# Sums of x's squares by ScalarE from a token-major copy of x, with h's row tiles and the memory's factors as jobs of their own

## The chip, the cores and the metric

The kernel runs on one core of one Trainium2 chip. The metric is the device time of the whole program in microseconds (us); several runs of a program are told by their median. TensorE (PE) does the matmuls, VectorE (DVE), ScalarE (ACT) and GpSimd (POOL) the elementwise work, and SyncE (SP) issues nearly all DMA transfers.

## What is computed

Two layers of an encoder trunk on x of 512 tokens by 1024 features, with 256 memory tokens beside it:

```python
for l in range(DEPTH):
    h = _rmsnorm(x, norm_g[l])
    u = h @ w_in[l]                 # one projection, split into the inputs of four head groups
    y_a = _hgrn2_branch(...)        # gated linear recurrence, both directions
    y_b = _window_attention(...)
    y_c = _mlstm_branch(...)
    y_d = _memory_attention(d_q, d_z, _rmsnorm(mem, mem_norm_g[l]), w_mem_kv[l])
    x = x + jnp.concatenate([y_a, y_b, y_c, y_d], axis=-1) @ w_out[l]
return _rmsnorm(x, final_norm_g)

def _rmsnorm(x, g):
    y = xf * lax.rsqrt(jnp.mean(xf * xf, axis=-1, keepdims=True) + EPS)
    return y * g
```

The change concerns the first layer's `_rmsnorm(x)` and `_rmsnorm(mem)`: the sum of squares over the 1024 features of each token, and what is made of it.

## The kernel before

Every float32 matrix product is done as three matmuls on a pair of parts, hi (the value rounded by a copy) and lo (the rest): hi·hi, hi·lo, lo·hi. Weights come from HBM in blocks of 512 rows by 256 columns (tile `wr`, three buffers); ACT copies a block to `wh`, DVE subtracts to `wl` (three buffers each), in `load_w`. x is loaded feature-major, as eight tiles `in_xT` of 128 features by 512 tokens (`xs`).

The program starts in `start()`. The normalised h needs a factor per token that isn't known until all of x has been squared, so the first projections run on h0, which is x times the gain without the factor, and the factor is multiplied on when the result is taken out of PSUM. For each of the eight feature tiles k the loop loads x and a piece of the first weight block, makes hi and lo of both, and issues six matmuls of the q projection into the two PSUM banks `o` (the tiles `pts`), 48 in all. In the same loop the squares are made: GpSimd squares the even tiles, ACT the odd ones, GpSimd and DVE add the eight squared tiles up into one (`plus`). Then a job R, written as a generator `rest()`, goes on:

- four matmuls of the summed tile with a column of ones (`add_squares`) give the token sums in PSUM (`tr`); `rms4` turns them into factors on ACT and DVE, `diag` puts them on a diagonal `dg`;
- after a yield, `spread` multiplies `dg` with a matrix of ones, so that every partition holds all the factors, and ACT copies this to R. DVE then multiplies the two q tiles by R, and `norm_k` makes h itself for k = 0 to 7: one multiplication by R (DVE for even k, GpSimd for odd k), hi by ACT, lo by DVE;
- the sums of the memory's squares were made by ACT from a token-major copy (`in_mem`); their `diag` and, after another yield, their `spread` into `Rm` close the job.

The forget gates of head group A are the first work that needs R. `gates()` does two projections of h0, one into the banks `s` (d = 1), one into `pj` (d = 0), and each result is multiplied by R on DVE before ACT's sigmoids. They are followed by `values()`, the first projection that needs h, and the two heads of `mix_A`: seven levels of a tree, each with small matmuls into the banks `s`, an update of K2 on GpSimd, one of Q2 on DVE, a masked copy on DVE. A job `memn` (`mem_norm`, `mem_kv`) multiplies the feature-major memory (`in_memT`) by gain and `Rm` on DVE and splits it into hi and lo.

Order: each engine runs its instructions in the order of its own stream, and SP its transfers likewise. `Weave` holds the jobs: the main line calls `tick` every few matmuls, which adds the time that they take by its plan, and a job whose due time (the `after` of its spawn, then the second number of each yield) has come runs a step. A framework then orders the instructions of each engine, where `tc.high_priority()` lets a piece go ahead; in the loop of `start()` the program's order is kept. So numbers such as `R_LAT` decide where in the streams a job's instructions stand.

Of the kernel before, what the change touches and what calls it, by code (L numbers as in the profile page):

```python
# [9 lines left out]
AF = mybir.ActivationFunctionType  # L10
# [4 lines left out]
P = 128  # L15
# [66 lines left out]
R_LAT0, R_LAT = 6000, 3500  # L82
M_LAT, M_LAT2 = 20000, 2500


def pack(inp):
# [18 lines left out]
    out = {"xT": inp["x"][0].T.reshape(8, P, T), "memT": inp["mem"][0].T.reshape(8, P, 256).transpose(1, 0, 2),  # L105
# [91 lines left out]
def trunk(tc, a, dbg=None, mark=lambda s: None):  # L197
# [6 lines left out]
    with es:  # L204
# [265 lines left out]
        def add_squares(ps, sq, n, first, last):  # L470

            for c in range(n):
                gmm(ps[:, c:c + 1], sq[:, c * P:(c + 1) * P], ones[:, 0:1], first and c == 0, last)

# [71 lines left out]
        jobM, mem0 = [], []  # L546
# [126 lines left out]
        def group_A(l, h, pr, yT, between=None, before=None, raw=None):  # L673
# [54 lines left out]
            if pr == 0:  # L728
                gates()
                if raw is not None:  # L730
                    jobM.append(wv.spawn("memn", mem_norm(), after=M_LAT))
# [464 lines left out]
        def mem_norm():  # L1196
            yield 0, 0
            mem0.append(mem_kv(0))
            next(mem0[0])
            yield 0, 0  # L1200
# [199 lines left out]
        def start():  # L1400
# [15 lines left out]
            sums = ptr()  # L1416
            pts = [po(), po()]
            R = a2([512])
            sqs = []

            def plus(e, i, j):
                e.tensor_tensor(sqs[i], sqs[i], sqs[j], ALU.add)
            for k in range(8):
# [19 lines left out]
                for b, pt in enumerate(pts):  # L1443
# [3 lines left out]
                    mm(pt, wl[:, c], hi, start=False, stop=(k == 7))  # L1447

            ms = a["mem"].rearrange("b (c p) d -> p (b c) d", p=P)
            ssm = sm([2], "ssm", 1)  # L1450
            mt = [u4([D]) for _ in range(2)]
            es2.close()
            for c in range(2):
                sy.dma_start(mt[c], ms[:, c])
# [117 lines left out]
```

## Time and profile before

| | |
|---|---|
| Median of 3 runs | 1136.97 us (1136.57 to 1139.35) |
| The profiled execution: its own time | 1137.1 us |
| The profiled execution: its span | 1135.3 us |
| PE busy | 1079.4 us, 95% |
| DVE busy | 795.3 us, 70% |
| ACT busy | 538.3 us, 47% |
| POOL busy | 243.4 us, 21% |
| Chain that ended last | PE 71%, DVE 18%, ACT 3% of the span |

The span is the time from the first to the last record; 1.8 us of the execution's own time lie around it. A time in a view counts from the start of the span. Busy shares average over very different stages: in the first 2.5% of the span PE is busy for six tenths, later for nearly all of it. What an edit is worth is to be read from the stage in which it lies. A PE that is busy can also be busy at half its pace: the clock granted is a column of its own.

### The profile page before, as it was taken

The page shows a single profiled execution, that of the slowest core. Times are in us where ns is not written, and L with a number is a line of the kernel's source. Part 1 is how long each engine was busy: PE and PEld are TensorE (multiplying, and loading weights), DVE is VectorE, ACT ScalarE, POOL GpSimd, SP SyncE. Part 2 cuts the span into 40 slices and gives each one's busy share as a digit, 9 for nine tenths or more (in the row PEclk, how much of TensorE's full clock was granted, in tenths as well). Part 3 has the DMA queues.
Part 4 walks back from the last instruction along what each step waited for, and adds up shares of the span by engine and source line. Part 5 has one row for each costly group of instructions (what it writes and reads, how often), then busy time and mean ns, then how long its engine had stood idle before and what let it go on. Part 6 is the DMA issues. An engine that isn't in the chain of part 4 may idle for free.

```text
span 1135.3 us, 22387 instructions
## 1 busy us (share of the span) xinstructions
PE 1079.4 (95%) x8886; PEld 968.2 (85%) x8886; DVE 795.3 (70%) x1759; ACT 538.3 (47%) x1138; POOL 243.4 (21%) x276
## 2 busy tenths in 40 slices
PE   6889999989999999999999999999899999999997
PEld 4778988989888888788788889889888788989997
DVE  7799536787486768777464786377968759688664
ACT  5545335666443534344564433376654353442443
POOL 4252000231142123111020241012304311230200
PEclk9999999999999999999999999999999999999998
DMA  7222134111221444422434221311121233362211
GB/s 255 77 94 76 57 104 158 59 57 45 88 75 58 108 107 122 148 76 92 134 128 142 81 67 58 98 62 56 58 75 57 76 108 98 103 195 77 74 38 74
DMA packets 34783, 105.41 MB, mean 93 GB/s; under 512 B 4360, under 2 KB 7816, under 8 KB 34680
## 3 DMA queue, kind: packets, MB, share of 16 engines
q1 hardware_dynamic: 33960, 101.57, 28.4%
q0 software_dynamic: 720, 2.42, 0.6%
q8 instruction: 70, 1.15, 0.4%
q14 instruction: 33, 0.27, 0.1%
HBM read 99.72 MB, written 4.26 MB: 92 GB/s over the span
## 4 chain that ended last, share of the span: by engine, by line
PE 71%; DVE 18%; ACT 3%; issue 2%; DMA 1%; POOL 0%; SPq 0%; DVEq 0%; ACTq 0%; POOLq 0%
PE pj L248 33%; PE pj L251 23%; DVE a L142 7%; DVE u L142 5%; PE o L248 4%; DVE wl L142 3%; PE s L248 3%; PE s L251 2%; ACT wh L142 1%; PE tr L857 1%; PE o L251 1%; ACT u L142 1%; ACT a L142 1%; DVE rq_t L142 1%; PE tr L1290 1%
## 5 line engine op out<-in xcount | busy, mean ns | idle before, releaser
L251 PE MATMUL pj<-wh,u 128*128 128x256 f32 x1984 | 390.7, 287 | 3.2 <-ACT u L142 1.2
L248 PE MATMUL pj<-u,wh 128*128 128x512 f32 (+1 forms) x1216 | 376.8, 391 | 1.0 <-ACT a L142 0.8
L251 PEld LDWEIGHTS pj<-wh,u 128*128 128x128 f32 x1984 | 317.0, 190 | 8.2 <-ACT u L142 2.4
L142 DVE TENSOR_TENSOR wl<-wr,wh 128x1024 fp32r<-128x1024 f32 (+1 forms) x162 | 215.4, 1330 | 135.8 <-ACT wh L142 135.3
L251 PE MATMUL pj<-wl,u 128*128 128x256 f32 x992 | 280.7, 283 | 0.0
L248 PEld LDWEIGHTS pj<-u,wh 128*128 128x128 f32 x1216 | 219.2, 190 | 42.5 <-ACT a L142 1.2
L248 PE MATMUL pj<-u,wl 128*128 128x512 f32 (+1 forms) x608 | 234.0, 385 | 1.8 <-DVE wl L142 1.8
L142 ACT CAST wh<-wr 128x1024 fp32r<-128x1024 f32 (+1 forms) x162 | 164.1, 1014 | 151.1 <-PE pj L248 88.0
L251 PEld LDWEIGHTS pj<-wl,u 128*128 128x128 f32 x992 | 188.3, 190 | 0.8 <-issue 0.3
L248 PEld LDWEIGHTS pj<-u,wl 128*128 128x128 f32 x608 | 115.4, 190 | 25.3 <-DVE wl L142 2.0
L142 POOL TENSOR_TENSOR u<-u,a 128x512 f32<-128x512 f32 (+1 forms) x64 | 93.2, 1464 | 133.0 <-PE s L251 53.5
L142 POOL TENSOR_SCALAR u<-u,rB 128x256 f32<-128x256 f32 (+1 forms) x64 | 37.3, 595 | 232.9 <-DVE rB L142 132.5
L142 POOL TENSOR_TENSOR u<-u,u 128x512 f32<-128x512 f32 x16 | 29.3, 1830 | 210.9 <-DVE a L142 125.0
L248 PE MATMUL pj<-wh,u 128*128 128x256 f32 (+1 forms) x320 | 62.8, 287 | 0.0
L142 DVE TENSOR_TENSOR u<-u,a 128x512 f32<-128x512 f32 (+1 forms) x56 | 50.2, 897 | 15.9 <-PE s L251 13.5
L248 PE MATMUL o<-u,u 128*128 128x129 f32 (+1 forms) x384 | 50.2, 275 | 1.9 <-DVE dnC L142 1.9
L248 PEld LDWEIGHTS o<-u,u 128*128 128x128 f32 x384 | 48.2, 191 | 4.4 <-issue 2.4
L248 PEld LDWEIGHTS pj<-wh,u 128*128 128x128 f32 x320 | 51.0, 188 | 0.7 <-issue 0.5
L251 PEld LDWEIGHTS s<-u,u 128*32 128x32 f32 (+1 forms) x1760 | 27.4, 115 | 28.1 <-issue 19.3
L251 PE MATMUL s<-u,u 128*32 128x32 f32 (+2 forms) x1760 | 35.0, 207 | 17.2 <-DVE a L142 13.6
L142 ACT COPY u<-u 128x512 f32<-128x512 f32 x40 | 27.0, 684 | 40.7 <-DVE u L142 22.8
L248 PE MATMUL pj<-wl,u 128*128 128x256 f32 (+1 forms) x160 | 45.3, 283 | 0.0
(213 smaller groups left out, 1494.3 us busy)
## 6 DMA issues: line engine op xcount, KB each, us to landing
wr<-in_wpk SPq DMA_DIRECT2D x154, 512.0 KB, 3.3
u<-in_xT SPq DMA_DIRECT2D x16, 256.0 KB, 4.6
u<-rdr SPq DMA_DIRECT2D x16, 256.0 KB, 4.5
u<-gdr SPq DMA_DIRECT2D x16, 192.0 KB, 5.8
u<-in_memT SPq DMA_DIRECT2D x4, 512.0 KB
xd<-u POOLq DMA_DIRECT2D x4, 512.0 KB, 4.8
u<-xd SPq DMA_DIRECT2D x4, 512.0 KB, 5.4
out<-u SPq DMA_DIRECT2D x8, 256.0 KB, 2.0
```

Of the source, the lines that this page charges most:

```text
L142: r = f(*args, **kw)
L248: nc.tensor.matmul(out, l, r, start=start, stop=stop)
L251: nc.tensor.matmul(out, l, r, start=start, stop=stop, skip_group_check=True)
L857: nc.tensor.transpose(pt[:, j * P:(j + 1) * P], pr[e][:, j * P:(j + 1) * P], ident)
L1290: nc.tensor.transpose(pt[:, (2 * t + i) * P:(2 * t + i + 1) * P], pr[:, i, t * P:(t + 1) * P], ident)
```

## The change

1. x is loaded a second time, token-major (`in_x`, four tiles of 128 tokens by 1024 features, 512 KB each), behind the first weight blocks and ahead of `in_mem`.
2. The squares and their additions leave the loop of `start()`, from GpSimd, ACT and DVE. ACT squares the four token-major tiles in `rest()`, and the sum over the features comes out of the same instruction (`accum_out`). The four matmuls with a column of ones are gone.
3. `norm_k` of the eight row tiles of h becomes a job N of its own, with one tile per step, and all eight multiplications by R are on DVE. `group_A` joins N ahead of `go()`.
4. The memory's `diag` is handed to the job `memn`, which does `spread` into `Rm` as its first step.
5. The due times that go with these jobs are others.

```diff
-R_LAT0, R_LAT = 6000, 3500
-M_LAT, M_LAT2 = 20000, 2500
+R_LAT0, R_LAT = 0, 9000
+H_LAT = 1100
+M_LAT, M_LAT2 = 20000, 1500
...
             if pr == 0:
                 gates()
+                wv.join(*jobN)
+                jobN.clear()
                 if raw is not None:
                     jobM.append(wv.spawn("memn", mem_norm(), after=M_LAT))
...
         def mem_norm():
             yield 0, 0
+            spread(jobM.pop(0), Rm)
+            yield 450, M_LAT2
             mem0.append(mem_kv(0))
...
-                sqs.append(a2([512]))
-                if k % 2 == 1:
-                    act.activation(sqs[k], x, AF.Square)
-                    if k < 6:
-                        plus(gp, k - 1, k)
-                else:
-                    gp.tensor_tensor(sqs[k], x, x, ALU.mult)
-                if k == 5:
-                    plus(dve, 0, 2)
-                elif k == 7:
-                    for j in (4, 6, 7):
-                        plus(dve, 0, j)
...
+            for name, ts in (("x", xt), ("mem", mt)):
+                src = a[name].rearrange("b (c p) d -> p (b c) d", p=P)
+                for c, t in enumerate(ts):
+                    sy.dma_start(t, src[:, c])
+
+            def squares(ts, ss):
+                for c, t in enumerate(ts):
+                    act.activation(t, t, AF.Square, accum_out=ss[:, c:c + 1])
             q = [a2([512]) for _ in range(2)]
 
             def rest():
 
+                squares(xt, sst)
                 with tc.high_priority():
-                    add_squares(sums, sqs[0], NC, True, True)
-                    dg = diag(rms4(sums[:, 0:NC]), NC)
-                yield 900, R_LAT
+                    dg = diag(rms4(sst), NC)
+                yield 0, R_LAT
                 with tc.high_priority():
                     spread(dg, R)
                     for b in range(2):
                         dve.tensor_tensor(q[b], pts[b], R, ALU.mult)
-                for k in range(8):
-                    norm_k(xs[k // 2][:, k % 2], k, R, 0, h, gp if k % 2 else dve)
-                for c in range(2):
-                    act.activation(mt[c], mt[c], AF.Square, accum_out=ssm[:, c:c + 1])
-                dg = diag(rms4(ssm, 2), 2)
-                yield 900, M_LAT2
-                spread(dg, Rm)
-                yield 450, 0
+                squares(mt, ssm)
+                jobM.append(diag(rms4(ssm, 2), 2))
+                jobN.append(wv.spawn("N", norms()))
+                yield 900, 0
+
+            def norms():
                 for k in range(8):
-                    norm_k(xs[k // 2][:, k % 2], k, R, 0, h, gp if k % 2 else dve)
+                    norm_k(xs[k // 2][:, k % 2], k, R, 0, h, dve)
+                    yield 0, H_LAT
```

How the streams differ, at three places. The rows are those of one engine in its own order, before and changed; `a_`, `u_` and so on are tiles with running numbers, which differ between the two.

PE where the q projection (`o`) ends and the gate projection d = 1 (`s`) begins; `tr_137` is the product with the column of ones. Before:

```order
L248 MATMUL o_139<-u_8_101,wl_129 128x512
L248 MATMUL s_277<-u_5_98,wh_266 128x512
L248 MATMUL s_277<-u_9_102,wh_266 128x512
L251 MATMUL tr_137<-ones,a_31_145 128x1 x4
L248 MATMUL s_277<-u_5_98,wl_267 128x512
```

and changed:

```order
L249 MATMUL o_138<-u_12_105,wh_128 128x512
L249 MATMUL o_138<-u_8_101,wl_129 128x512
L249 MATMUL s_262<-u_5_98,wh_251 128x512
L249 MATMUL s_262<-u_9_102,wh_251 128x512
L249 MATMUL s_262<-u_5_98,wl_252 128x512
```

The product with the ones, which stood two matmuls into the gate projection, is gone; the `spread` matmul now follows 19 matmuls into that projection, where before it stood 11 in.

DVE from the factors of x on (before: `a_60_322` is their diagonal; `a_30_140` is R, `a_62_335` and the next three are the even tiles' products with R). Before:

```order
L142 TENSOR_TENSOR a_60_322<-cf,rx_57_313 128x512
L142 TENSOR_TENSOR wl_405<-wr_403,wh_404 128x4x256
L142 TENSOR_TENSOR a_42_249<-o_138,a_30_140 128x512
L142 TENSOR_TENSOR a_43_250<-o_139,a_30_140 128x512
L142 TENSOR_TENSOR a_62_335<-u_1_94,a_30_140 128x512
L142 TENSOR_TENSOR a_64_343<-u_2_95,a_30_140 128x512
L142 TENSOR_TENSOR a_66_351<-u_3_96,a_30_140 128x512
L142 TENSOR_TENSOR a_68_359<-u_4_97,a_30_140 128x512
L142 TENSOR_TENSOR wl_411<-wr_409,wh_410 128x4x256
```

and changed (`a_29_139` is R, `s_262` the first gate result, `a_61_331` the diagonal of the memory's factors):

```order
L143 TENSOR_TENSOR a_38_234<-o_137,a_29_139 128x512
L143 TENSOR_TENSOR a_39_235<-o_138,a_29_139 128x512
L143 RECIPROCAL rx_58_322<-rx_58_322 128x2
L143 TENSOR_TENSOR rxv_59_323<-rxv_59_323,rx_58_322 128x2
L143 TENSOR_TENSOR wl_363<-wr_361,wh_362 128x4x256
L143 SCALAR_TENSOR_TENSOR rxt_60_324<-rxv_59_323,rx_58_322 128x2
L143 SCALAR_TENSOR_TENSOR rx_58_322<-rxt_60_324,rx_58_322 128x2
L143 TENSOR_TENSOR a_61_331<-cf,rx_58_322 128x256
L143 TENSOR_TENSOR wl_369<-wr_367,wh_368 128x4x256
L143 TENSOR_TENSOR a_62_333<-s_262,a_29_139 128x512
L143 TENSOR_TENSOR a_63_340<-u_1_94,a_29_139 128x512
L143 TENSOR_TENSOR a_64_350<-u_1_94,a_29_139 128x512
```

The memory's factors, `wl` of two blocks and the first gate result moved ahead of the products of x with R, and those are eight instead of four.

DVE among the levels of `mix_A` (`u_121`, `u_122`, in the change `u_119`, `u_120`: the feature-major memory; updates of Q2 have forms such as 128x128x2x2). Before, ahead of the update by the second level:

```order
L142 TENSOR_TENSOR a_101_520<-a_101_520 128x8
L142 SCALAR_TENSOR_TENSOR u_121_849<-u_121_849,pg,Rm 128x256 x3
L142 TENSOR_TENSOR u_96_494<-u_96_494,a_42_249 128x128x2x2
L142 COPY_PREDICATED a_99_499<-cu,s_679 128x128
L142 TENSOR_TENSOR wl_992<-wr_990,wh_991 128x4x256
L142 TENSOR_TENSOR u_100_519<-u_100_519,a_43_250 128x128x2x2
L142 COPY_PREDICATED a_103_524<-cu,s_729 128x128
L142 SCALAR_TENSOR_TENSOR u_121_849<-u_121_849,pg,Rm 128x256
```

and changed, ahead of the update by the fifth level:

```order
L143 TENSOR_SCALAR rk_938<-ang 128x32
L143 SCALAR_TENSOR_TENSOR u_119_871<-u_119_871,pg,Rm 128x256
L143 SCALAR_TENSOR_TENSOR u_110_696<-a_126_931,pj_698 128x512
L143 TENSOR_TENSOR wl_1221<-wr_1219,wh_1220 128x4x256
L143 SCALAR_TENSOR_TENSOR u_119_871<-u_119_871,pg,Rm 128x256 x3
L143 SCALAR_TENSOR_TENSOR u_120_872<-u_120_872,pg,Rm 128x256 x3
L143 TENSOR_TENSOR u_123_875<-u_119_871,u_121_873 128x1024
L143 SCALAR_TENSOR_TENSOR u_120_872<-u_120_872,pg,Rm 128x256
L143 TENSOR_SCALAR rk_938<-rk_938 128x32
L143 TENSOR_TENSOR u_91_476<-u_91_476,a_92_477 128x16x2x16
```

The products with `Rm` start three levels later; the result that frees the PSUM bank `pj_698` and the block `wl_1221` stand among them. In SP's stream the two transfers of `in_memT` moved two weight blocks back, to behind `wr_1461`.

## Rows read from the trace of the kernel before

**Rows 1.** Busy time by stage: window; PE, PEld, DVE, ACT, POOL; clock, DMA, GB/s.
```profile
23.10:26.50 3.40, 1.51 (x11) 1.07 (x10) 2.71 (x6) 0.00 (x0) 0.00 (x0) 1.00 0.73 219
26.50:31.40 4.90, 4.90 (x15) 3.55 (x15) 2.76 (x11) 1.45 (x4) 0.00 (x0) 0.65 0.34 106
...
43.90:47.00 3.10, 0.13 (x1) 0.02 (x1) 3.10 (x6) 0.00 (x0) 0.00 (x0) 1.00 0.04 13
47.00:51.20 4.20, 4.19 (x12) 3.33 (x13) 1.26 (x3) 3.45 (x5) 0.00 (x0) 0.59 0.36 115
...
65.00:92.00 27.00, 20.36 (x384) 18.50 (x383) 26.86 (x43) 11.62 (x18) 11.81 (x8) 1.00 0.30 99
...
110.00:1135.00 1025.00, 989.15 (x7939) 891.49 (x7937) 701.77 (x1596) 481.88 (x1045) 200.50 (x242) 0.99 0.29 89
```

**Rows 2.** PE's waits up to 110 us: waiter, releaser: sum, times, longest.
```profile
PE s L251 <- DVE a L142: 5.4, 3, 3.4
PE tr L248 <- DVE a L142: 3.0, 1, 3.0
PE tr L251 <- DVE a L142: 1.9, 1, 1.9
```

**Rows 3.** PE in order of time: start, us, instruction, count, idle before.
```profile
13.72 0.39 PE L248 MATMUL o<-u,wl 128*128 128x512 f32 x1
...
22.21 0.40 PE L248 MATMUL o<-u,wl 128*128 128x512 f32 x1
...
22.91 0.39 PE L248 MATMUL o<-u,wl 128*128 128x512 f32 x1
...
26.54 0.48 PE L248 MATMUL s<-u,wl 128*128 128x512 f32 x1
...
56.04 0.28 PE L251 MATMUL pj<-wh,u 128*128 128x256 f32 x1
```

**Rows 4.** DVE and POOL in order of time during the q projection.
```profile
9.12 0.41 DVE L142 TENSOR_TENSOR wl<-wr,wh 128x256 fp32r<-128x256 f32 x1
...
14.02 1.26 DVE L142 TENSOR_TENSOR wl<-wr,wh 128x256 fp32r<-128x256 f32 x1
...
13.51 1.49 POOL L142 TENSOR_TENSOR a<-u 128x512 f32<-128x512 f32 x1
```

**Rows 5.** The same columns as rows 1, for the loads ahead of the memory's.
```profile
11.25:13.50 2.25, 2.25 (x7) 1.71 (x7) 2.25 (x2) 2.25 (x6) 2.17 (x2) 1.00 1.08 393
```

**Rows 6.** ACT and DVE in order of time: squares with sum, factors, R.
```profile
18.84 1.06 ACT L142 ACTIVATE u<-u 128x1024 f32<-128x1024 f32 x1
...
19.80 0.19 ACT L142 ACTIVATION_READ_ACCUMULATOR u<-u 128x1 f32 x1
...
26.72 0.26 ACT L142 ACTIVATE rx<-tr,epst 128x4 f32<-128x4 f32 x1 [6.73 <-PE tr L251]
...
28.29 0.69 DVE L142 TENSOR_TENSOR a<-cf,rx 128x512 f32<-128x512 f32 x1 [0.34 <-DVE rx L142]
...
31.34 0.59 ACT L142 COPY a<-tr 128x512 f32<-128x512 f32 x1 [3.24 <-PE tr L248]
```

**Rows 7.** DVE in order of time with GpSimd idle: lo of h, wl, results.
```profile
40.02 4.71 DVE L142 SCALAR_TENSOR_TENSOR u<-a,pg,u 128x512 fp32r<-128x512 f32 x7
44.66 1.21 DVE L142 TENSOR_TENSOR wl<-wr,wh 128x1024 fp32r<-128x1024 f32 x1
...
46.79 1.27 DVE L142 TENSOR_TENSOR a<-s,a 128x512 f32<-128x512 f32 x2
```

**Rows 8.** POOL, DVE and SP in order of time around the levels of mix_A.
```profile
61.28 2.94 POOL L142 TENSOR_TENSOR u<-u,u 128x512 f32<-128x512 f32 x1 [0.69 <-DVE a L142]
...
63.00 2.29 DVE L142 TENSOR_TENSOR wl<-wr,wh 128x1024 fp32r<-128x1024 f32 x1 [0.73 <-ACT wh L142]
...
75.80 2.17 DVE L142 SCALAR_TENSOR_TENSOR u<-u,pg,Rm 128x256 f32<-128x256 f32 x3
...
65.70 0.91 SPq L142 DMA_DIRECT2D u<-in_memT  x2
```

More of the change, by code (lines that the diff above doesn't have):

```diff
@@ L104, in pack @@
     cf, cu = const_arrays()
-    out = {"xT": inp["x"][0].T.reshape(8, P, T), "memT": inp["mem"][0].T.reshape(8, P, 256).transpose(1, 0, 2),
+    out = {"x": inp["x"], "xT": inp["x"][0].T.reshape(8, P, T), "memT": inp["mem"][0].T.reshape(8, P, 256).transpose(1, 0, 2),
            "mem": inp["mem"], "pos": inp["positions"].reshape(NC, P).T, "pg": pg, "final_norm_g": inp["final_norm_g"], "wpk": np.stack(ws).reshape(-1, P, 1024), "wg": wg.reshape(NL, P, P),
@@ L468, in rms @@
             return r
-        def add_squares(ps, sq, n, first, last):
-            for c in range(n):
-                gmm(ps[:, c:c + 1], sq[:, c * P:(c + 1) * P], ones[:, 0:1], first and c == 0, last)
         def rms4(ss, n=NC):
@@ L545, in trunk @@
         last_exp = []
-        jobM, mem0 = [], []
+        jobM, jobN, mem0 = [], [], []
         def mix_A(l, hd, F2, K2, q, v, gz, yT):
@@ L1415, in start @@
                 sy.dma_start(ws[-1][0][:, k % 4], a["wpk"][k // 4][:, 256 * (k % 4):256 * (k % 4) + 256])
-            sums = ptr()
             pts = [po(), po()]
             R = a2([512])
-            sqs = []
-            def plus(e, i, j):
-                e.tensor_tensor(sqs[i], sqs[i], sqs[j], ALU.add)
             for k in range(8):
@@ L1447, in start @@
                     mm(pt, wl[:, c], hi, start=False, stop=(k == 7))
-            ms = a["mem"].rearrange("b (c p) d -> p (b c) d", p=P)
-            ssm = sm([2], "ssm", 1)
-            mt = [u4([D]) for _ in range(2)]
             es2.close()
-            for c in range(2):
-                sy.dma_start(mt[c], ms[:, c])
+            xt, mt = [[u4([D]) for _ in range(n)] for n in (NC, 2)]
+            sst, ssm = [sm([n], t, 1) for t, n in (("sst", NC), ("ssm", 2))]
+            for name, ts in (("x", xt), ("mem", mt)):
[5 more added lines that the diff above has]
+                    act.activation(t, t, AF.Square, accum_out=ss[:, c:c + 1])
             q = [a2([512]) for _ in range(2)]
             def rest():
+                squares(xt, sst)
                 with tc.high_priority():
-                    add_squares(sums, sqs[0], NC, True, True)
-                    dg = diag(rms4(sums[:, 0:NC]), NC)
-                yield 900, R_LAT
+                    dg = diag(rms4(sst), NC)
+                yield 0, R_LAT
                 with tc.high_priority():
@@ L1466, in rest @@
                         dve.tensor_tensor(q[b], pts[b], R, ALU.mult)
-                for k in range(8):
-                    norm_k(xs[k // 2][:, k % 2], k, R, 0, h, gp if k % 2 else dve)
-                for c in range(2):
-                    act.activation(mt[c], mt[c], AF.Square, accum_out=ssm[:, c:c + 1])
-                dg = diag(rms4(ssm, 2), 2)
-                yield 900, M_LAT2
-                spread(dg, Rm)
-                yield 450, 0
+                squares(mt, ssm)
[3 more added lines that the diff above has]
+            def norms():
+                for k in range(8):
+                    norm_k(xs[k // 2][:, k % 2], k, R, 0, h, dve)
+                    yield 0, H_LAT
             return h, (q, h0, R, wv.spawn("R", rest(), after=R_LAT0))
```

## The prediction

> **What bounds the kernel now.** I read the page first, then PE's waits, then busy time by stage, then the streams in order of time where PE stands. The page puts PE at 95% of the span. From 110 us to the end PE is busy for 989 of 1025 us [rows 1], and the streams of all engines keep their order from about there on, so I take what PE gains ahead of 110 us as gained at the end, and look for nothing else behind it. Ahead of it PE's time goes in three ways:
>
> - It stands while the squares are summed: 1.9 us for DVE's last addition, and 3.0 us for the diagonal of the memory's factors, which waits in DVE's stream behind the lo parts of h [rows 2].
> - After each of these stops it runs at half its pace: the clock granted is 0.65 of full in the stretch from 26.5 to 31.4 us and 0.59 in that from 47.0 to 51.2 us, so for most of each the lower of its two levels, 1.2 GHz [rows 1].
> - From 65 to 92 us it is busy for 20.4 of 27 us, while DVE is busy for 26.9 [rows 1]: PE waits there for DVE in the levels of mix_A, 5.4 us in three waits alone [rows 2]. In this stage DVE is the bound.
>
> I call the start of the value projection, the first work on h, V. It is at 56.04 us [rows 3]. The working has two terms: how much earlier V comes, and what PE's waits behind V become.
>
> **Term 1, up to V.**
>
> *The q projection.* GpSimd's squares and sums cost nothing on GpSimd but stretch DVE: the same subtraction takes 0.41 us at 9.12 us and 1.26 us at 14.02 us, where it ends just after a GpSimd operation that began before it [rows 4]. So DVE falls behind PE. From 13.72 us to the gate projection 34 of the 48 matmuls are left, the last of them at 22.91 us; at full pace three take 22.91 − 22.21 = 0.70 us [rows 3], so 34 take 7.9 us, and the last would end at 21.6 instead of 23.1 us: 1.5 us. Without GpSimd and the additions, DVE needs about 1.0 us per feature tile and PE 1.4, so DVE no longer holds PE. The cover for ACT is as wide, since its four squares leave the loop too.
>
> *The column sums.* The matmuls of the ones are gone with the wait ahead of them. Two gate matmuls behind 23.1 us PE was free at 23.6; the next one starts at 26.54 [rows 3]: 2.9 us.
>
> *Half pace.* By the granted clock PE loses 0.35 × 4.9 = 1.7 us of full-pace work in the first of the two stretches and 0.41 × 4.2 = 1.7 us in the second [rows 1]: 3.4 us. I take both as gone with the stops, as in these rows nothing but a stop stands ahead of the fall of the clock.
>
> *The second stop.* The memory's diagonal now stands ahead of the products of x with R in DVE's stream, and its spread at the end of the gate projections: 3.0 us.
>
> Sum 10.8 us. Counted the other way, from 21.6 us with 96 gate matmuls at 0.231 us and the two spreads at 0.5 together, PE would be through at 21.6 + 22.2 + 0.5 = 44.3 us, 11.7 ahead of V; the 0.9 us more lie in matmuls next to the stops that the windows cut. I go on with the count. Against it stands what R and h need in their new place.
>
> *The second load of x.* It adds 2.1 MB to a stretch in which the DMA engines are full, at 393 GB/s [rows 5]. By then 3.0 MB are loaded, counted from the same view; up to x's last tile 3.6 MB more have to come, so it lands at 11.25 + 3.6/0.39 = 20.5 us, and what follows (the memory, `cu`, the next weights) 5.4 us later than it would. Those weights land at about 25 us and are wanted at 33.
>
> *The squares on ACT.* Each takes 1.06 us and a read of the sum that ends at 19.99, so 1.25 us from start to start with what lies between [rows 6]. Four tiles as they land: the last sum at 21.8 to 22.4 us. From the root at 26.72 to the end of the diagonal at 28.98 it took 2.3 us [rows 6]; so the diagonal is there at 24.1 to 24.7. PE comes to the spread 19 matmuls into the gate projection, at 21.6 + 4.4 = 26.0 us: hidden, with 1.3 us to spare. R follows after the spread and ACT's copy of 0.59 us at about 27.3 us, instead of 31.93.
>
> *h on DVE alone.* This is what decides V. From R on DVE has: two q tiles and two gate results, at 0.6 us; the rest of the memory's factors, 1.2 us; four blocks of wl at 1.13 up to the eighth product; eight products with R at 0.6; seven lo at 0.67; the third gate result, which frees the PSUM bank that V needs [rows 7]. That is 2.4 + 1.2 + 4.5 + 4.8 + 4.7 + 0.65 = 18.3 us, from 27.3 to 45.6 us. PE is through at 44.3. So V waits some 1.3 us, for the DVE stream, and comes at about 45.7 us: 10.3 us earlier than before. GpSimd's four products cost DVE little: before, DVE's own four were stretched beside them. Bounds: 45.0 us if the blocks of wl find their PSUM and buffers free at once, 47.5 us if ACT's hi parts, which now stand behind two copies of weights that wait for PE, come late; so 8.5 to 11 us.
>
> **Term 2, the levels.** Behind V DVE has the same operations as before, but the eight products with `Rm`, three of which take 2.17 us [rows 8], and the two subtractions that split the memory, as long as a block of wl (1.21 us [rows 7]), 6 to 8 us in all, leave the stretch in which PE waited for it and come three levels later. The longest wait, 3.4 us [rows 2], was for an update that stood right behind those three; with them gone I let 0.8 us of it remain. The other two waits of that kind are 2.0 us together; I keep 1.1, for the one that lies ahead of the products. The rest of the 6.6 us that PE isn't busy from 65 to 92 us [rows 1] goes. At the fifth and sixth level, where the products now stand, I allow as much new waiting as the rows show in the two short waits, less what the order gives back, 1.7 us. So 6.6 becomes 3.6, and the term is 3.0 us; bounds: −1 (all the waits stay, with one more) to 6.6.
>
> GpSimd's update of K2 and DVE take turns there: the block of wl at 63.00 us took 2.29 us instead of 1.21, and ended 1.1 us behind the end of the GpSimd operation begun at 61.28 [rows 7, 8]. After V the first updates and DVE's products now come at the same time. The Trainium skill ("SBUF — State Buffer", section "SBUF: two separate sides") says that GpSimd and a DVE operation with two SBUF inputs share a pair of ports that is locked for a whole instruction, and that the other fully blocks. By that rule the times simply add up, and the chain of levels starts later behind V; the trace agrees for the row at 63.00. It is the first rival's mechanism.
>
> **Sum.** 1137.1 − 10.3 − 3.0 = 1123.8 us. The profiled execution, 1137.1 us, is 0.1 us above the median, so both serve as the base.
>
> **Rivals.**
>
> *The levels give nothing back.* DVE's products and two GpSimd updates of 1.9 us each, all at once behind V, add up to some 6.7 us from the point at which the first update can start, 1.2 us later relative to V than before, and PE, which comes to each level sooner, waits that much more. For it: DVE is full there [rows 1]. Against: the products with `Rm` are out of the way. Only term 1 stays: 1137.1 − 10.3 + 0.5 = 1127.3 us.
>
> *A stop takes the place of the old ones.* If x lands 3 us later than worked out, or h's parts come late, PE stops for 2 us ahead of the spread or of V, and after that runs at half pace, as after the 1.9 us stop [rows 1, 2]: 2 + 2 us, and 1 us less at the levels: 1137.1 − 13.3 + 5 = 1128.8 us. The rows give 1.3 us to spare for the one; V has none.
>
> *The memory's transfer blocks DVE: slower.* The products with `Rm` wait for `in_memT`, which is issued behind the weight block `wr_1461`, and that waits for its buffer. Behind the first product in DVE's stream stand the result that frees PE's bank and the next wl. Before, the transfer was issued at 65.70 us and its first product came at 75.80 [rows 8], with ten microseconds between; now I count 1 MB and a weight block in front of about 3 us. A late transfer costs its lateness beyond that, one for one, and the half pace behind it. From some 13 us of lateness on the whole gain is gone; at 17 us the time is about 1141 us. The load itself takes 4 us at the rate of [rows 5], so only a held queue would do it; I find none.
>
> **Chances.** Forecast 0.62 (1119.5 to 1127), levels give nothing 0.20, a new stop 0.13, slower 0.05. The range should take in the first two and most of the third: 1119.5 (term 1 at 11, term 2 at 6.6) to 1129.5 us. Faster by over 0.3%, which is 3.4 us and about what a measurement of this kernel can tell from no change: 0.92; within: 0.04; slower: 0.04.
>
> **What would show it.** In the profile of the changed kernel: no DVE operation of the q projection above 0.8 us, and the gate projection's first matmul at 21.5 to 22 us; the last ACT square ending by 22.5; no stop of PE between there and 44 us, and the granted clock at full throughout; R by 27.5; V at 45 to 46.5 us with a wait of 1 to 2 us for DVE; PE's waits between V and 55 us behind it at 3 to 4 us; behind that the same distances as before. It would be wrong if PE stops ahead of the spread, if V lies behind 47.5, or if DVE waits for a DMA among the products with `Rm`.

## The result, and the profile after

| | before | changed |
|---|---|---|
| Median | 1136.93 us (4 runs) | 1129.1 us (4 runs, 1126.78 to 1130.45) |
| Ratio, 95% interval | 1 | 0.9925 (0.9903 to 0.9946) |
| The profiled execution: its own time | 1137.1 us | 1130.45 us |
| V, first matmul of the value projection | 56.04 us | 45.21 us |
| First transposes of K2, behind the levels | 109.9 us | 99.6 us |
| First output matmul behind the levels (`o`) | 113.99 us | 104.86 us |
| PE busy, DVE busy | 1079.4, 795.3 us | 1079.0, 785.9 us |

The change is faster by 0.75%, 7.8 us; 13.3 were forecast. Two more measurements of the same kernel, below, gave ratios of 0.9903 and 0.993; the median of all its twelve executions is 1128.6 us, that of 42 executions of the kernel before 1137.5: 8.9 us.

Term 1 can be read off three views. PE's stream in order of time (start, duration, line, operation, idle time ahead of it and what ended it). Before, the gate projection began at 23.14 us, with a stop in it [rows 2], and V stood at 56.04 [rows 3]:

```profile
23.14 0.62 PE L248 MATMUL s<-u,wh 128*128 128x512 f32 x2
```

Changed:

```profile
20.66 0.63 PE L249 MATMUL s<-u,wh 128*128 128x512 f32 x2
...
25.07 1.02 PE L249 MATMUL tr<-a,ones 128*128 128x512 f32 x2
...
45.21 0.35 PE L252 MATMUL pj<-wh,u 128*128 128x256 f32 x1 [0.81 <-ACT Rm L143]
```

The spread (`tr`) finds its diagonal ready, and V waits 0.8 us. The view names ACT's copy of `Rm` (44.77 to 45.13 us) as what ended this wait; DVE's third gate result, which frees V's bank, ended at 45.06, so the two are too close to tell apart. ACT's stream, with the first and last square, the last read of a sum, and R:

```profile
17.11 1.06 ACT L143 ACTIVATE u<-u 128x1024 f32<-128x1024 f32 x1
...
20.91 1.06 ACT L143 ACTIVATE u<-u 128x1024 f32<-128x1024 f32 x1
21.87 0.18 ACT L143 ACTIVATION_READ_ACCUMULATOR u<-u 128x1 f32 x1
...
26.13 0.59 ACT L143 COPY a<-tr 128x512 f32<-128x512 f32 x1 [1.50 <-PE tr L249]
```

Busy time by stretch, the windows of [rows 1] (the third number from the end is the granted clock): the two that stood at 0.65 and 0.59 are at full clock.

```profile
26.50:31.40 4.90, 4.90 (x23) 3.96 (x22) 4.55 (x10) 3.57 (x5) 0.00 (x0) 1.00 0.30 76
...
47.00:51.20 4.20, 4.20 (x38) 4.20 (x38) 3.93 (x5) 2.45 (x5) 2.51 (x1) 1.00 0.40 125
65.00:92.00 27.00, 22.93 (x380) 21.15 (x378) 24.21 (x42) 10.84 (x16) 10.68 (x6) 1.00 0.30 101
```

Behind V the gain grows at first and is then lost. PE's waits in the levels:

```profile
57.65 0.54 PE L252 MATMUL s<-u,u 128*32 128x32 f32 x32 [2.38 <-DVE a L143]
...
67.30 0.46 PE L252 MATMUL s<-u,u 128*32 128x32 f32 x32 [0.34 <-DVE a L143]
...
70.96 0.46 PE L252 MATMUL s<-u,u 128*32 128x32 f32 x32 [1.59 <-DVE a L143]
...
87.97 0.46 PE L252 MATMUL s<-u,u 128*32 128x32 f32 x32 [1.59 <-DVE rr L143]
```

With two of 0.69 and 0.68 us at 92.2 and 94.8 these are 7.3 us; before there were four waits, 6.4 us in all (three of [rows 2] and one of 1.0). Matched matmul by matmul, the changed kernel is 10.8 us ahead at V, 13.4 at 78.3 us, behind the first three of these waits, and 10.2 at the transposes: the last three waits take back more than the levels had given until then. Another 1.1 us goes between the transposes and `o`. Before:

```profile
109.88 0.82 PE L632 MATMUL tr<-cf,u 128*128 128x128 f32 x6
...
113.99 2.39 PE L248 MATMUL o<-u,u 128*128 128x128 f32 x20
```

Changed, with a row of ACT's stream between the two of PE's:

```profile
99.64 0.82 PE L628 MATMUL tr<-cf,u 128*128 128x128 f32 x6
...
101.48 1.28 ACT L143 ACT_TABLE_LOAD   x1
...
104.86 0.38 PE L249 MATMUL o<-u,u 128*128 128x128 f32 x2
```

ACT loads a table of functions there, between its copies of the transposes that PE waits for; before, that load stood at 98.79 us, ahead of them. And the streams of DVE, POOL and SP in the levels:

```profile
52.22 1.74 DVE L143 TENSOR_TENSOR wl<-wr,wh 128x1024 fp32r<-128x1024 f32 x1 [1.28 <-ACT wh L143]
53.87 2.49 DVE L143 TENSOR_TENSOR a<-u 128x512 f32<-128x512 f32 x1
...
72.83 2.13 DVE L143 TENSOR_TENSOR wl<-wr,wh 128x1024 fp32r<-128x1024 f32 x1
...
80.67 0.48 DVE L143 SCALAR_TENSOR_TENSOR u<-u,pg,Rm 128x256 f32<-128x256 f32 x1 [2.32 <-DMA u<-in_memT]
```

```profile
48.69 7.13 POOL L143 TENSOR_TENSOR u<-u,u 128x512 f32<-128x512 f32 x2 [45.31 <-ACT u L143]
```

```profile
29.48 45.84 SPq L143 DMA_DIRECT2D wr<-in_wpk  x8
75.36 1.75 SPq L143 DMA_DIRECT2D u<-in_memT  x2
```

DVE waits 2.3 us for the memory; its transfer was issued at 75.4, as SP stood until then at the weight block in front of it. That block, issued at 74.98, waited for a buffer which DVE's own subtraction (`wl`, 72.83 to 74.96) frees. And two updates of K2 by GpSimd come in one piece of 7.1 us, beside which a DVE product that takes 0.7 us alone takes 2.5.

So V came 10.8 us earlier, the output matmul behind the levels 9.1, and at the last matmul into `pj`, at 1120.65 us instead of 1127.04, 6.4 were left. Three questions: where 1.7 us were lost from V to `o` instead of 3.0 gained, what was lost behind them, and whether the steps of term 1 hold one by one.

### The profile page after: what moved, and what is told of

Read it like the earlier page. It is cut to its first block, busy times and chain, and to the rows that moved or that the text cites. A ratio compares the mean times of both kernels' runs of the same rounds, so it can differ in the third digit from the quotient of the medians.

```text
span 1128.7 us, 22366 instructions
## 1 busy us (share of the span) xinstructions
PE 1079.0 (96%) x8878; PEld 970.1 (86%) x8878; DVE 785.9 (70%) x1759; ACT 541.7 (48%) x1142; POOL 229.2 (20%) x265
## 4 chain that ended last, share of the span: by engine, by line
PE 67%; DVE 22%; ACT 5%; issue 3%; DMA 2%; POOL 1%; SPq 0%; DVEq 0%; ACTq 0%; POOLq 0%
PE pj L249 30%; PE pj L252 21%; DVE a L143 8%; DVE u L143 6%; PE o L249 5%; DVE wl L143 5%; PE s L249 4%; ACT wh L143 2%; PE s L252 2%; ACT u L143 2%; PE tr L855 1%; ACT a L143 1%; PE o L252 1%; DMA u<-in_memT 1%; DVE rq_t L143 1%
## 5 line engine op out<-in xcount | busy, mean ns | idle before, releaser
L143 DVE TENSOR_TENSOR wl<-wr,wh 128x1024 fp32r<-128x1024 f32 (+1 forms) x162 | 213.1, 1316 | 135.3 <-ACT wh L143 134.4
L143 POOL TENSOR_TENSOR u<-u,u 128x512 f32<-128x512 f32 x16 | 30.7, 1922 | 238.7 <-DVE a L143 104.9
L252 PEld LDWEIGHTS s<-u,u 128*32 128x32 f32 (+1 forms) x1760 | 27.4, 115 | 28.5 <-issue 17.5
L252 PE MATMUL s<-u,u 128*32 128x32 f32 (+2 forms) x1760 | 34.9, 207 | 17.5 <-DVE a L143 12.3
```

Of the source, the lines that this page charges most:

```text
L143: r = f(*args, **kw)
L252: nc.tensor.matmul(out, l, r, start=start, stop=stop, skip_group_check=True)
```

## The experiments

Each ratio is to the kernel before on the same chip; V, the way and `o` are from the profiled execution, in us. "Falls" counts the stretches behind 110 us, the program's end left out, in which the granted clock of the profiled execution is at the lower level (the kernel before: three in each of its two traces).

| | V | V to transposes of K2 | `o` | falls | median, us | ratio (95%) |
|---|---|---|---|---|---|---|
| changed | 45.2 | 54.4 | 104.9 | 7 | 1129.1 | 0.9925 (0.9903 to 0.9946) |
| again | 45.0 | 54.5 | 104.7 | 2 | 1126.7 | 0.9903 (0.9884 to 0.9922) |
| again_b | 45.1 | 54.7 | 105.0 | 2 | 1129.8 | 0.993 (0.9908 to 0.9952) |
| memT_early | 45.6 | 52.1 | 102.2 | 5 | 1125.3 | 0.9898 (0.987 to 0.9925) |
| products_late | 45.7 | 51.3 | 101.0 | 6 | 1123.7 | 0.9882 (0.9864 to 0.99) |
| tables_early | 52.6 | 56.0 | 113.0 | 5 | 1133.3 | 0.9961 (0.9948 to 0.9973) |
| k2_on_dve | 45.2 | 53.1 | 103.5 | 5 | 1126.7 | 0.9899 (0.9884 to 0.9913) |
| late_and_k2 | 45.9 | 49.3 | 99.2 | 5 | 1123.8 | 0.9876 (0.9861 to 0.9891) |
| h_half_gpsimd | 43.8 | 55.7 | 104.7 | 7 | 1128.7 | 0.9913 (0.9896 to 0.9929) |
| all_three | 43.9 | 50.6 | 98.5 | 1 | 1119.8 | 0.9844 (0.9829 to 0.9859) |
| shift_1_6us | 44.7 | 50.6 | 99.4 | 6 | 1125.5 | 0.9885 (0.9864 to 0.9906) |
| squares_alone | 47.5 | 55.7 | 107.3 | 5 | 1130.6 | 0.9939 (0.9923 to 0.9955) |

### The late transfer

`mem_load` allocates the two tiles and issues their transfers, here ahead of the weights of the value projection; `hold[0]` is the masked copy of the fourth level, head 1. `M_LAT` is 22000 in this run; the diff leaves that out, and the definition of `mem_load`.

```diff
+                    memT0.append(mem_load())
                     jobM.append(wv.spawn("memn", mem_norm(), after=M_LAT))
...
-                    dve.scalar_tensor_tensor(v, v, gm[:, l, 4 * i + k:4 * i + k + 1], Rm, ALU.mult, ALU.mult)
+                    with tc.issue_after(hold[0]) if l == 0 else contextlib.nullcontext():
+                        dve.scalar_tensor_tensor(v, v, gm[:, l, 4 * i + k:4 * i + k + 1], Rm, ALU.mult, ALU.mult)
```

> The transfer of the feature-major memory is issued three weight blocks earlier; the products with Rm are held at the place in DVE's stream where the changed kernel has them, behind the masked copy of the fourth level. Only the wait of DVE for in_memT (2.32 us) can go. My theory, that the levels' stage is bound by DVE's stream, and that this wait ate part of the forecast gain: no DVE wait for in_memT, and the way from V to the first transposes of K2 behind the levels falls from 54.4 to about 52.5 us, PE's wait of 1.6 us at the fifth level being gone. The rival, that the chain through GpSimd, ACT and PE sets that stage and DVE's wait stood beside it: the way stays at 54.4 within 0.4 us.

SP's stream and DVE's, at the same place as above:

```profile
41.34 0.90 SPq L143 DMA_DIRECT2D u<-in_memT  x2
```

```profile
77.96 0.30 DVE L143 COPY_PREDICATED a<-cu,s 128x128 f32<-128x128 uint8 x1
78.16 1.27 DVE L143 SCALAR_TENSOR_TENSOR u<-u,pg,Rm 128x256 f32<-128x256 f32 x3
```

No wait stands ahead of the products. Of PE's three waits from the fifth level on, 3.0 us together, one of 0.74 is left, and the way is 52.1 us: shorter by 2.3 us, the length of DVE's wait. The rival falls.

```diff
-M_LAT, M_LAT2 = 20000, 1500
+M_LAT, M_LAT2 = 36000, 1500
```

> The job of the memory starts 16 us later by its plan, so that its transfer, the eight products with Rm and the two splits stand behind all levels of mix_A on DVE. The theory (DVE is the bound in the levels): with 5.7 us of products and splits and 2.3 us of waiting gone from ahead of them, all of PE's waits from the fifth level on go, 3.0 us, and the way from V to the transposes falls from 54.4 to about 51.5 us; the end gains up to that unless the memory's projections then wait for the parts. The rival (the chain through GpSimd, ACT and PE sets it): 54.4 within 0.5 us. My prediction's rival, a late transfer that blocks DVE, would show here as a new DVE wait for in_memT behind the levels.

The products now stand at 97.2 us on DVE, without a wait ahead of them:

```profile
97.16 3.20 DVE L143 SCALAR_TENSOR_TENSOR u<-u,pg,Rm 128x256 f32<-128x256 f32 x7
```

The way is 51.3 us, 3.2 shorter than in the changed kernel and 2.6 shorter than before (53.8), where term 2 forecast 3.0. Of the 3.2 the wait makes 2.3 and the products and splits themselves, 5.7 us of DVE's time, only 0.9. The memory's projections behind didn't wait for it; a product behind `o` did wait 0.84 us for DVE.

```diff
+            if l == 0:
+                setup2()
             jobs = group_A(l, h, 0, yA, raw=raw)
-            if l == 0:
-                setup2()
```

> The position tables and the gates' lower bound (some 30 small DVE operations, about 5 us from 77.8 to 101 us, and two sines on ACT) are written ahead of head group A instead of behind it, so that they leave the levels' stage. DVE-bound theory: the way from V to the transposes falls by 1 to 2.5 us from 54.4, V moves by less than 0.7 us, since DVE has idle time in the gate projections. Rival: the way stays, and V comes later by what the tables cost in the start.

The tables are written there ahead of everything else on DVE, and this spoilt the start, so the run decides nothing on the levels. ACT's sines, which wait for DVE, came to stand ahead of the first hi part, and PE's first matmul at 13.36 us instead of 6.5. One row shows the transfer's part again: DVE reached the products 33.0 us behind V (33.1 in the changed kernel) and waited 4.1 us, since the transfer, issued 30.5 us behind V, took 6.5 us until the first product could begin, against 5.3 in the changed kernel:

```profile
89.71 0.48 DVE L143 SCALAR_TENSOR_TENSOR u<-u,pg,Rm 128x256 f32<-128x256 f32 x1 [4.08 <-DMA u<-in_memT]
```

### GpSimd beside DVE

```diff
-                gp.tensor_tensor(k2v, k2v, V(Tm, n + 1, [[2, n // 2], [-(n + 1), 2], [0, m]]), ALU.mult)
+                (dve if m == 1 and l == 0 and hd < 2 else gp).tensor_tensor(k2v, k2v, V(Tm, n + 1, [[2, n // 2], [-(n + 1), 2], [0, m]]), ALU.mult)
```

> The changed kernel with the first level's update of K2 for both heads on DVE instead of GpSimd. In the changed kernel these two GpSimd operations take 7.1 us in one piece, and beside them a DVE product takes 2.49 us instead of 0.68 and a block of wl 1.74 instead of 1.22; PE waits 2.38 us at the first level right behind them. If the collision is what makes that wait: the product back at 0.7, the wl at 1.2, PE's wait at the first level 1.2 to 1.8 in spite of 2.1 us more work on DVE, and V to the transposes 53.4 instead of 54.4. If DVE's own work is the bound there and GpSimd only gets in its gaps: the 2.1 us show, PE's wait is 2.4 or longer, V to the transposes 54.4 to 56.

DVE's stream; the two updates are its first row here:

```profile
50.83 2.11 DVE L143 TENSOR_TENSOR u<-u,u 128x512 f32<-128x512 f32 x2
52.77 1.22 DVE L143 TENSOR_TENSOR wl<-wr,wh 128x1024 fp32r<-128x1024 f32 x1
53.91 0.67 DVE L143 TENSOR_TENSOR a<-u 128x512 f32<-128x512 f32 x1
```

The wl is back from 1.74 to 1.22 us, the product from 2.49 to 0.67, and PE's wait at the first level is 0.65 instead of 2.38 us. DVE did 2.1 us more work and was through 1.8 us sooner. The way shrank by 1.35 us, more than expected. This fits the port lock of the first rival (the Trainium skill, "SBUF — State Buffer", section "SBUF: two separate sides"). The trace agrees: in the changed kernel GpSimd's second update ended at 55.82 us, and the DVE product that had begun at 53.87 only behind it, at 56.36.

> The memory's job 16 us later (as in products_late, where V to the transposes took 51.3 us) and the first level's update of K2 on DVE. If both gains are real and independent, V to the transposes is 50.3 us and the end 4 us ahead of the changed kernel at the same number of falls of the clock; if the collision is no cost, 51.3.

The way is 49.3, 5.1 us shorter than in the changed kernel, so both gains are real. But the median, 1123.8, is that of `products_late` (1123.7), although `o` comes 1.8 us earlier than there; the falls below are why medians a few us apart don't rank these kernels.

```diff
-                    norm_k(xs[k // 2][:, k % 2], k, R, 0, h, dve)
+                    norm_k(xs[k // 2][:, k % 2], k, R, 0, h, gp if k % 2 else dve)
```

> The changed kernel with every second product of x and R on GpSimd again, jobs and order as changed. My prediction had DVE's stream decide V (DVE alone makes h) and held GpSimd's four products to cost DVE little. By that V comes up to 0.8 us earlier (its wait for the bank goes) and the last gate results and with them GpSimd's first update of K2 up to 2.4 us (four products of 0.6) earlier; DVE operations beside a GpSimd product stay below 1.0 us where 0.7 is normal. The rival: a GpSimd product holds DVE up, as in the row at 63 us of the kernel before (2.29 instead of 1.21); then the lo parts are stretched, V comes 1 to 3 us later and nothing is gained.

POOL's and DVE's streams:

```profile
48.24 9.94 POOL L143 TENSOR_TENSOR u<-u,u 128x512 f32<-128x512 f32 x2 [15.37 <-ACT u L143]
```

```profile
28.09 1.23 DVE L143 TENSOR_TENSOR rxv<-rxv,rx 128x2 f32<-128x2 f32 x1
...
54.26 5.55 DVE L143 TENSOR_TENSOR a<-a 128x256 f32<-128x256 f32 x3
```

V came 1.45 us earlier, without a wait. Of that 0.8 is the wait, and 0.6 is the memory's spread, two matmuls that stand ahead of V in the changed kernel and at 73.6 us here; that DVE's stream decided V is shown for the 0.8 at most. And GpSimd's first update of K2 began only 0.45 us earlier, the two took 9.9 us, and three small DVE products 5.55 (0.97 us in the changed kernel); at `o` 0.2 us were left. A DVE operation on two columns, 0.16 us in the changed kernel, took 1.23 us beside GpSimd, and there are three of them: "cost DVE little" left these out. V is not the landmark that the end hangs on.

> Late memory's job, first level's update of K2 on DVE, and every second product of h on GpSimd. With GpSimd's products alone V came 1.45 us earlier and the levels gave it back, since the two updates of K2 on GpSimd then took 9.9 us beside a fuller DVE. With these updates on DVE that cannot happen: if the levels hang on when DVE gets to ks, Q2 and K2, V is at 44.4, the wait at the first level stays under 1 us, and the transposes come at 93 to 94 us (95.2 with late_and_k2). If the levels hang on something else, they stay at 95.2 although V is earlier.

The second case holds: the earlier V isn't kept. The transposes come at 94.5 us, 0.7 ahead of `late_and_k2`, but 0.6 of that is an earlier start (gate projection at 20.71 instead of 21.32 us). From there the transposes take 73.8 us in both, though V takes 23.15 here and 24.55 there. PE's wait at the first level, expected under 1 us, is 1.59; in `all_three` and in `late_and_k2`:

```profile
55.52 0.54 PE L252 MATMUL s<-u,u 128*32 128x32 f32 x32 [1.59 <-DVE a L143]
...
56.58 0.54 PE L252 MATMUL s<-u,u 128*32 128x32 f32 x32 [0.64 <-DVE a L143]
```

The median is 1119.8 us, 17.5 us (1.6%) under the kernel before, and of the versions run here the fastest. As `o` is only 0.7 us ahead of `late_and_k2`, some 3.3 of the 4.0 us between the two medians come behind it, where the trace has one fall instead of five. How much of that is luck is the matter of the next section.

### The steps of term 1, and the falls of the clock

The squares alone, with h's tiles and the memory's diagonal in the job R as before:

```diff
-                squares(mt, ssm)
-                jobM.append(diag(rms4(ssm, 2), 2))
-                jobN.append(wv.spawn("N", norms()))
...
+                for k in range(8):
+                    norm_k(xs[k // 2][:, k % 2], k, R, 0, h, gp if k % 2 else dve)
+                squares(mt, ssm)
+                dg = diag(rms4(ssm, 2), 2)
+                yield 900, 2500
+                spread(dg, Rm)
...
```

> One part of the change alone: the squares by ScalarE from the token-major copy. The row tiles of h (every second product on GpSimd) and the memory's diagonal and spread are back in the job R as in the kernel before. My steps for term 1: this part brings the earlier end of the q projection, the column sums and the first half pace (1.5 + 2.9 + 1.7 us less what R needs), the other part brings the second stop with its half pace. So R at 26.7 as in the changed kernel, the stop of about 3 us ahead of the second spread and the granted clock at half behind it still there, V at about 50.8 us (before it stood 24.1 us behind R), and V to the transposes as before, 53.9. The rival, that the second stop stood only because the first one had let DVE fall behind: V near 46 without these parts, and they bring nothing.

The second stop is there, and behind it the clock stays full (PE's stream, then the stretch behind):

```profile
44.88 0.70 PE L249 MATMUL tr<-a,ones 128*128 128x256 f32 x2 [2.53 <-DVE a L143]
```

```profile
45.00:49.00 4.00, 4.00 (x24) 3.56 (x25) 2.71 (x5) 2.11 (x3) 0.00 (x0) 1.00 0.32 120
```

So the second stop does go with the other part of the change, the job N and the diagonal's place, which were not tried apart. And the half pace isn't tied to a stop as my sum had it: V at 47.5, not 50.8. Of these 3.3 us the half pace makes 1.7. Most of the rest fits 8 matmuls, 1.8 us, by which the gate projection is further on when the spread comes; that is an estimate. V to the transposes, expected as before, is 55.7 us instead of 53.8, with a wait of 3.2 us at the first level. By the medians this part alone brings 7.0 us.

> The kernel before once more, unedited. In its first trace the granted clock fell to half behind both early stops of PE (1.9 and 3.0 us), and my term 1 counts 3.4 us for that as gone with the stops. In the run with the squares alone a stop of 2.5 us ahead of the spread had no fall behind it. If a fall follows every such stop, both are there again in this trace, behind 26.5 and 47 us, and V is at 56.0 within 0.3 us. If a stop is only where a fall may come, one or both are missing, and V is 1.7 us earlier for each; then part of the 3.4 us was of that one execution, and the stops' places in the program repeat while V does not.

Both stops repeat (1.89 and 2.96 us; 1.89 and 2.99 in the first trace), but only behind the second does the clock fall. The stretches behind the first and the second:

```profile
28.00:32.00 4.00, 3.83 (x15) 2.50 (x14) 3.23 (x5) 0.62 (x2) 1.35 (x2) 1.00 0.29 85
...
46.00:50.00 4.00, 4.00 (x12) 3.13 (x12) 0.73 (x2) 3.07 (x4) 0.00 (x0) 0.64 0.28 112
```

V stands at 54.65 here, 1.4 us earlier than in the first trace; 0.2 of that is an earlier gate projection. (Median 1136.8 us, ratio 1.0001.)

> The changed kernel once more, unedited. In its first trace the granted clock is at half for seven short stretches behind 110 us, where the kernel before has three, and none ahead of it. If these falls are what separates its executions, the places up to the transposes behind the levels repeat within 0.3 us (V at 45.2, first transposes of K2 at 99.6), the number or the places of the later falls are others, and the span differs by up to 1.7 us (0.5 x 3.4) for each that is more or less. If instead the later falls belong to the changed order, the same seven come back at the same instructions.

> The changed kernel a third time, on the same chip as the kernel before. By the two traces so far: V at 45.1, first transposes of K2 at 99.5, each within 0.3 us unless a fall lies ahead of them; three to seven falls behind 110 us; median 9 to 11 us under the kernel before.

The same kernel three times: the places up to `o` repeat within 0.4 us, the later falls don't (seven, two, two), and the last matmul into `pj` begins at 1120.65, 1114.96 and 1116.83 us. The median of `again_b` is 7.5 us under the kernel before, not the 9 to 11 expected. Both repeats also have a fall in the levels, at 59 us, which the first trace hasn't: PE's waits behind it shrink from 1.9 to 0.8 us, and from V to `o` it costs 0.3 us at most. Stops of PE between the mixers come at the same places of the program each time; whether the clock falls behind one differs. One of them, at 1002 us of the changed kernel's first trace, PE's stream and the stretch behind:

```profile
1002.63 0.38 PE L252 MATMUL pj<-wh,u 128*128 128x256 f32 x1 [0.97 <-ACT a L143]
...
1004.33 1.44 PE L249 MATMUL o<-u,u 128*128 128x129 f32 x8 [0.73 <-DVE dnC L143]
```

```profile
1004.30:1008.40 4.10, 4.07 (x22) 4.10 (x23) 2.79 (x8) 2.37 (x5) 0.37 (x1) 0.58 0.88 341
```

And the same place in the kernel before:

```profile
1010.39 0.39 PE L251 MATMUL pj<-wh,u 128*128 128x256 f32 x1 [0.81 <-ACT a L142]
...
1012.09 1.13 PE L248 MATMUL o<-u,u 128*128 128x129 f32 x8 [0.71 <-DVE dnC L142]
```

```profile
1012.00:1016.10 4.10, 4.01 (x35) 4.05 (x36) 2.81 (x9) 2.32 (x5) 0.42 (x1) 1.00 0.85 318
```

35 matmuls there, 22 here. Between the first trace and `again` five falls make 5.7 us less the 0.2 us at `o`: 1.1 us each on the average. Matched matmul by matmul they differ, from 1.6 us at 449 us to nothing at 640, where the time lost came back at two waits of PE that shrank from 0.35 and 1.59 us to 0 and 0.91. Against `again_b` five falls make 4.0 us, 0.8 each. The last kernel asks whether they belong to an order of instructions or to when a stop comes:

```diff
+            if l == 0:
+                pt = ptr()
+                for k in range(7):
+                    mm(pt, w[0](0)[:, 0:P], rows(h[0], 0), start=(k == 0), stop=(k == 6))
             gz = [gate_ch(h, load_w(2)) for _ in range(2)]
```

> The kernel of all_three with seven more matmuls (128x512, nobody reads their result) ahead of the z gates of group B, where PE is busy without a gap: everything behind is 7 x 0.231 = 1.6 us later, at otherwise the same order. In all_three the mean clock was 0.995 to 0.997 in all four executions and one fall stood between 110 us and the last group, where the changed kernel had three to seven. If whether a stop is followed by a fall hangs on when it comes and not on what the stop is, the falls change in number or place and the end moves by another amount than 1.6 us: by 1.6 + about 1.2 for each additional fall, 4 to 8 us later with three to five of them. If few falls belong to the order of all_three, the clock stays at 0.995 and the end comes 1.6 us later, within 0.7 us.

Two of the places in `all_three`:

```profile
573.00:583.00 10.00, 7.84 (x64) 7.43 (x64) 10.00 (x12) 6.17 (x11) 0.56 (x1) 1.00 0.46 156
787.00:797.00 10.00, 7.35 (x63) 7.00 (x62) 9.28 (x19) 4.29 (x9) 3.68 (x6) 1.00 0.16 56
```

and in the shifted kernel, with a fall in each:

```profile
579.00:589.00 10.00, 8.20 (x57) 8.00 (x56) 10.00 (x13) 5.81 (x10) 0.23 (x1) 0.83 0.46 157
793.00:803.00 10.00, 7.39 (x51) 7.22 (x50) 9.79 (x20) 3.50 (x7) 3.86 (x6) 0.83 0.15 56
```

(The changed kernel had two to seven falls behind 110 us in its three traces, not three to seven as expected here.) 1.6 us of matmuls cost 5.7 us at the median; apart from them one weight block's copy and subtraction moved by a few places. In the traces the shifted kernel is 0.8 us later at V already, 2.6 behind the added matmuls, and 7.7 at the last matmul into `pj`; the steps in between lie at the falls, six against one. The four executions of `all_three` have a mean clock of 0.995 to 0.997 and the five of the shifted kernel 0.987 to 0.996; the one at 0.996 took 1121.6 us, which is `all_three` and the added work. So the few falls don't belong to the order of `all_three`: the shifted kernel has nearly the same order and more of them in most executions. That the shift made them isn't shown. The two kernels ran on different chips, and the unedited changed kernel has seven falls in one trace and two in the others.

## Why the prediction was right in part

*Term 1 (10.3 us; V came 10.8 earlier in the first trace).* The steps hold: the gate projection's first matmul at 20.7 (21.6 forecast), the last square's sum read by 22.1 (22.4), the spread without a wait at 25.1 (26.0), R copied by 26.7 (27.3), full clock to 110 us in the first trace, V at 45.2 with a wait of 0.8 us (45.7 with 1.3). What I had as certain and is not is the 3.4 us of half pace: a stop can have it behind it or not. Against the second trace of the kernel before V gains 9.4 us; 10.3 lies between.

*Term 2 (+3.0 us; from V to `o` it was -1.7).* This is the step that failed. I left 3.6 of 6.6 us of waiting: 1.1 at the first level, 0.8 at the next, 1.7 at the fifth and sixth. It is 2.38, then 0.34 + 1.59, then 1.59 + 0.69 + 0.68: 7.3, so 3.7 us of the 4.7 by which the term is off. Three mis-sized parts, each with its run, and a term that I had at nothing:

- *"1 MB and a weight block in front of about 3 us", for the memory's transfer.* I counted its place in SP's queue and the time of the blocks ahead, not that the block ahead waits for a buffer that DVE itself frees, late in its full stream. DVE came to the products at 78.35 us, 3.4 behind the end of that subtraction, and the transfer took 5.3 us from its issue to the first product. The prediction's own sign, DVE waiting for a DMA among the products with `Rm`, is in the trace. I had the mechanism as a rival at 0.05, for a lateness of 13 us and more; 2.3 us of it came, and `memT_early` gives them back whole.
- *The collision of GpSimd and DVE behind V.* I named it and gave it 0.20, as the case in which the levels give nothing back. It came in addition: moving the updates to DVE gives back 1.35 us.
- *V as the point from which the levels count.* GpSimd's first update waits for ACT, which needs the last gate results from DVE, and these stand behind h's products: it began at 48.69 us, 3.5 behind V. Before, the two were apart (the second is in [rows 8]) and the first began 1.6 behind V; POOL's stream there:

```profile
57.67 2.92 POOL L142 TENSOR_TENSOR u<-u,u 128x512 f32<-128x512 f32 x1 [19.25 <-DVE a L142]
```

  So that start gained 9.0 us, not 10.8. `h_half_gpsimd` and `all_three` show the same the other way round: V earlier, the levels not.
- *Nothing behind the levels.* From the transposes to `o` it is 5.2 us instead of 4.1, with ACT's table load among the copies of the transposes. The traces go together with that: 5.2 us in all five in which the load stands between ACT's copies of the transposes (the changed kernel's three, `k2_on_dve`, `h_half_gpsimd`), 4.1 to 4.5 in the other nine. No run moves the load alone.

Most of the gain that I had expected in the levels was there to be had: `products_late` has 2.6 of the 3.0 us. But of its 3.2 us over the changed kernel most hung on the transfer, not on the products.

*"The streams of all engines keep their order from about there on, so I take what PE gains ahead of 110 us as gained at the end."* The order is kept, the time isn't: of 9.1 us at `o` the first trace has 6.4 at the last matmul into `pj`; `again`, with 9.3 at `o`, has 12.1. The kernel before has falls there as well, and over all executions the gain at the end, 8.9 us, is about that at `o`, 9.1; so on the average this neither gives nor takes much, but for one median of four it is some 2 us. The time of the forecast missed by 5.3 us; 4.7 are term 2, -0.5 term 1, and the rest, about 1, is what this leaves. The measured 1129.1 us lies outside the stretch that I gave 0.62, and 0.4 us inside the end of the whole range, which the rivals had set; `again_b`, the same kernel, lies outside it at 1129.8. That the time fell into the range is in part luck.

*The rivals.* The nearest in time is the second, 1128.8 us, but its mechanism, a new stop ahead of the spread or V, didn't come. The first, 1127.3 us, and the third each have their mechanism in the trace, the third with 2.3 us of lateness that cost DVE time instead of 13 and more.

**What stays open.** The waits of 1.6 us at the third level are the same in `memT_early`, `products_late` and `k2_on_dve` and 0.6 in `all_three`, behind two of 0.4 and 0.7 for ACT; whether GpSimd's later updates make them wasn't tried. What the levels hang on, if not on V, isn't shown. Why one execution has a fall behind most stops and another of the same order behind few stays open: it isn't the order alone, as the three traces of one kernel show. That it is when the stops come is argued, not shown.

## What to carry to other kernels

- When work on one engine is made earlier, go through the transfers that it needs: each keeps its place in its queue, behind blocks that wait for their buffers, here for one that the waiting engine itself frees. Issue the transfer with the work's new place, not with its old one.
- Follow the gain to what the next stage starts from. Here it was not the matmul that I had chosen as the landmark: two kernels with an earlier V reached the transposes no earlier. And a GpSimd operation that runs beside a chain of DVE operations is paid by the chain.
- Before a difference of a few us is believed, compare places in the traces ahead of and behind the edit and count the falls of the clock in each. Unedited repeats, and an experiment that only shifts the program, show what the noise of an edit is.

## What the runs showed of the hardware

- Two stops of PE close together, 0.97 and 0.73 us, are enough that the granted clock may fall to the level of 1.2 GHz behind them (0.58 as the mean of the next 4.1 us); a stop of 2.5 us had none behind it, and one of 1.9 us had it in one of two traces of the same kernel. The number of falls isn't the program's alone: one kernel had seven, two and two in three traces, and `all_three` one, with 1.6 us of added matmuls six.
- A fall costs some 0.8 to 1.1 us at the end here, on the average of five; the one at 640 us of the first trace, where DVE is busy throughout, moved nothing behind it by more than 0.1 us, as PE's waits shrank by what it lost. The falls at 59 us of the two repeats cost 0.3 us at most.
- Beside a GpSimd product a DVE operation with two inputs in SBUF waits, however small: 1.23 us instead of 0.16 for two columns, 5.55 instead of 0.97 us for three products of 256 columns and fewer. GpSimd is stretched too: two updates took 9.9 us beside a full DVE, 7.1 beside a less full one.
